# RMSNorm with SiLU: a first block of four rows, last blocks of four and two, and the first store behind the squares of block 1

## The chip, the cores and the metric

The kernel runs on one core of a Trainium2 chip. The time is device microseconds for one execution; a lower one is better. A core has five engines that run side by side: TensorE (PE), VectorE (DVE), ScalarE (ACT), GpSimd (POOL) and SyncE (SP). Data moves between the chip's main memory (HBM) and the on-chip memory (SBUF) through 16 DMA engines, which all transfers of the core share. A transfer is issued by an instruction on an engine's queue; here SP issues all loads and ACT all stores.

## The reference

The input x is 8 x 1024 x 2048 in float32, that is 8192 rows of 2048 numbers (8 KB each, 67.1 MB in all). Each row is divided by its root mean square, multiplied by gamma, and passed through SiLU. The output has the size of the input.

```python
def reference(x, gamma, eps):
    rms = np.sqrt(np.mean(x ** 2, axis=-1, keepdims=True) + eps)
    out = gamma * x / rms
    return (out * (1 / (1 + np.exp(-out)))).astype(np.float32)
```

## The kernel before

The 8192 rows are 64 for each of the 128 partitions. They are cut into blocks: a block of J rows covers 128 x J consecutive rows of x, and partition p holds J consecutive ones, so that one partition's piece is J x 8 KB of contiguous memory. Before the change there are eleven blocks: ten of six rows (48 KB per partition, 6 MB in all) and one of four (32 KB, 4 MB).

A pool of four buffers of six rows holds the blocks (`BUFS = 4`). `load(b)` (line 59) issues one transfer on SP, `store(b, j0, j1)` (line 66) one on ACT. Every block is computed in place and stored from the buffer it was loaded into. A load into a buffer thus waits until the store of the block that was in it has completed: load b + 4 waits for store b.

`work(b)` is one block's computation, in program order:

- ACT squares the first half of the rows and sums each (line 73, a Square with an accumulated output into `ss`); DVE does the same for the other half by a multiply and reduce (line 75).
- ACT takes the square root of the mean square plus eps for all rows of the block (line 80); DVE takes the reciprocal (line 85).
- For each row DVE multiplies by gamma, held on every partition as `g` (line 83), and ACT applies Silu with the reciprocal as its scale (line 86). DVE's half of the rows goes first.
- ACT issues the store of the block; in the last block in two halves, the first of them as soon as its rows are done. Then SP issues the load of block b + 4.

[...]

At the start the loads of blocks 0, 1 and 2 are issued. Gamma comes in as four pieces on ACT's queue into the fourth buffer, is spread over the partitions by four matmuls (line 111) and copied to `g` (line 113); then the load of block 3 goes into that fourth buffer (its load waits for the matmuls).

The order on each engine is the program's order: the whole kernel is under a manual schedule. So what ACT does before a store is issued is all that stands before it in the program, and a load on SP stands behind all loads issued before it.

Of the kernel before, what the change touches and what calls it, by code (L numbers as in the profile page):

```python
# [1 line left out]

# [4 lines left out]

ACT = mybir.ActivationFunctionType
ALU = mybir.AluOpType


@with_exitstack
def kernel(
    ctx: ExitStack,
    tc: tile.TileContext,
    x: bass.AP,
    gamma: bass.AP,
    eps: bass.AP,
    out: bass.AP,
):  # L20

    nc = tc.nc
    P = nc.NUM_PARTITIONS
    f32 = mybir.dt.float32
    x2 = x.flatten_outer_dims()
    o2 = out.flatten_outer_dims()  # L30
    n, d = x2.shape
    JMAX, BUFS = 6, 4
    blks = []
    r = 0
    while r < n:
        j = JMAX if n - r >= JMAX * P else 4
        blks.append((r, j))
        r += j * P
    nblk = len(blks)

    def rows_of(t, b):
        r0, J = blks[b]
        return t[r0:r0 + P * J, :].rearrange("(p j) d -> p (j d)", p=P, j=J)

    singles = ctx.enter_context(tc.tile_pool(name="singles", bufs=1))
    pool = ctx.enter_context(tc.tile_pool(name="pool", bufs=BUFS))
    small = ctx.enter_context(tc.tile_pool(name="small", bufs=2))
    psum = ctx.enter_context(tc.tile_pool(name="psum", bufs=1, space=bass.MemoryType.PSUM))

    g = singles.tile([P, d], f32)  # L50
    eps_t = singles.tile([P, 1], f32)
    ones = singles.tile([P, P], f32)
    junk_a = psum.tile([P, d], f32, name="junk_a")
    junk_v = psum.tile([P, d], f32, name="junk_v")
    blocks = {}

    def load(b):
        xt = pool.tile([P, JMAX * d], f32, name="xt")
        nc.sync.dma_start(out=xt[:, 0:blks[b][1] * d], in_=rows_of(x2, b))  # L59
        blocks[b] = xt  # L60

    def row(b, j):
        return blocks[b][:, j * d:(j + 1) * d]

    def store(b, j0, j1):
        nc.scalar.dma_start(out=rows_of(o2, b)[:, j0 * d:j1 * d], in_=blocks[b][:, j0 * d:j1 * d])  # L66

    def work(b):
        J = blks[b][1]
        A = J // 2  # L70
        ss = small.tile([P, JMAX], f32, name="ss")
        for j in range(A):
            nc.scalar.activation(out=junk_a, in_=row(b, j), func=ACT.Square, accum_out=ss[:, j:j + 1])  # L73
        for j in range(A, J):
            nc.vector.tensor_tensor_reduce(  # L75
                out=junk_v, in0=row(b, j), in1=row(b, j), scale=1.0, scalar=0.0,
                op0=ALU.mult, op1=ALU.add, accum_out=ss[:, j:j + 1])
        rms = small.tile([P, JMAX], f32, name="rms")
        rstd = small.tile([P, JMAX], f32, name="rstd")
        nc.scalar.activation(out=rms[:, 0:J], in_=ss[:, 0:J], func=ACT.Sqrt, scale=1.0 / d, bias=eps_t)  # L80
        order = list(range(A, J)) + list(range(A))
        for i, j in enumerate(order):
            nc.vector.tensor_mul(out=row(b, j), in0=row(b, j), in1=g)  # L83
            if i == 0:
                nc.vector.reciprocal(out=rstd[:, 0:J], in_=rms[:, 0:J])  # L85
            nc.scalar.activation(out=row(b, j), in_=row(b, j), func=ACT.Silu, scale=rstd[:, j:j + 1])  # L86
            if b == nblk - 1 and i == J - A - 1:
                store(b, A, J)
        if b == nblk - 1:
            store(b, 0, A)  # L90
        else:
            store(b, 0, J)
        if b + BUFS < nblk:
            load(b + BUFS)

    with tc.manual_schedule():


        Q = 4
        w = d // Q  # L100
        grow = pool.tile([P, JMAX * d], f32, name="xt")
        for b in range(BUFS - 1):
            load(b)
        nc.vector.memset(ones, 1.0)  # L104
        nc.vector.memset(eps_t, float(eps))  # L105
        nc.scalar.activation(out=junk_a[:, 0:1], in_=ones[:, 0:1], func=ACT.Square)  # L106
        nc.scalar.dma_start(out=grow[0:P:P // Q, 0:w],
                            in_=bass.AP(tensor=gamma.tensor, offset=gamma.offset, ap=[[w, Q], [1, w]]))
        for c in range(Q):
            k = c * (P // Q)  # L110
            nc.tensor.matmul(junk_v[:, c * w:(c + 1) * w], ones[k:k + 1, :], grow[k:k + 1, 0:w],  # L111
                             start=True, stop=True)
        nc.vector.tensor_copy(out=g, in_=junk_v)  # L113
        load(BUFS - 1)
        for b in range(nblk):
            work(b)


# [1 line left out]
_INS = ['x', 'gamma', 'eps']  # L120
_OUTS = [((8, 1024, 2048), 'float32')]

_NUMBERS = {'eps': 9.999999747378752e-06}


# [26 lines left out]
```

## Time and profile before

| | |
|---|---|
| median of 11 runs | 317.32 us (317.17 to 318.49) |
| the profiled execution | 317.3 us, of which the span of its instructions is 315.5 us |
| VectorE busy | 218.9 us, 69% of the span |
| ScalarE busy | 222.4 us, 70% of the span |
| gamma product, line 83 | 64 rows, 2277 ns each, 142.4 us |
| Silu, line 86 | 64 rows, 1996 ns each, 125.3 us |
| reduction on VectorE, line 75 | 32 rows, 2299 ns each; waits 59.8 us for loads |
| square on ScalarE, line 73 | 32 rows, 1882 ns each and 186 ns to read its sum; waits 56.6 us for loads |
| table loads on ScalarE | 11 before Sqrt and 11 before Silu, 1283 ns each |
| a load of 6 MB | median 35.1 us from issue to landing |
| a store of 6 MB | median 45.9 us from issue to landing |

The profile is one execution. Its span reaches from the first instruction to the last; the time has about 2 us more, outside the span. "Busy" is the share of the span in which an engine worked. In rows with a square bracket, the bracket holds the time for which the engine was idle before this instruction, and what released it. The DMA share of a stretch is the mean busy share of the 16 DMA engines, and the rate beside it is what they moved; both are counted by whole packets, of up to 48 KB here, so short stretches swing (a share can pass 1).

### The profile page before, as it was taken

The page shows a single profiled execution, that of the slowest core. Times are in us where ns is not written, and L with a number is a line of the kernel's source. Part 1 is how long each engine was busy: PE and PEld are TensorE (multiplying, and loading weights), DVE is VectorE, ACT ScalarE, POOL GpSimd, SP SyncE. Part 2 cuts the span into 40 slices and gives each one's busy share as a digit, 9 for nine tenths or more (in the row PEclk, how much of TensorE's full clock was granted, in tenths as well). Part 3 has the DMA queues.
Part 4 walks back from the last instruction along what each step waited for, and adds up shares of the span by engine and source line. Part 5 has one row for each costly group of instructions (what it writes and reads, how often), then busy time and mean ns, then how long its engine had stood idle before and what let it go on. Part 6 is the DMA issues. An engine that isn't in the chain of part 4 may idle for free.

```text
span 315.5 us, 421 instructions
## 1 busy us (share of the span) xinstructions
PE 2.1 (1%) x8; PEld 0.5 (0%) x8; DVE 218.9 (69%) x142; ACT 222.4 (70%) x163; POOL 0.2 (0%) x4
## 2 busy tenths in 40 slices
PE   0200000000000000000000000000000000000000
PEld 0000000000000000000000000000000000000000
DVE  0269998989989099539926990996299269959100
ACT  1068999999999289738956892898289568978400
POOL 0000000000000000000000000000000000000000
DMA  8999999999999999999999999999999999999997
GB/s 306 480 411 411 474 349 461 399 436 461 400 450 442 405 455 436 405 461 430 405 486 411 418 474 405 424 467 405 436 455 405 442 430 436 415 459 437 405 422 310
DMA packets 3323, 134.25 MB, mean 426 GB/s; under 512 B 372, under 2 KB 372, under 8 KB 376
## 3 DMA queue, kind: packets, MB, share of 16 engines
q1 hardware_dynamic: 1584, 67.11, 49.8%
q10 hardware_dynamic: 1736, 67.12, 49.2%
q14 instruction: 3, 0.02, 0.0%
HBM read 67.12 MB, written 67.11 MB: 425 GB/s over the span
## 4 chain that ended last, share of the span: by engine, by line
another core or an unknown queue 36%; DMA 31%; DVE 15%; ACT 9%; issue 1%; SPq 0%; ACTq 0%; DVEq 0%
DMA out_dram<-xt 16%; DMA xt<-in_x_dram 15%; DVE xt L83 11%; ACT xt L86 4%; DVE junk_v L75 4%; ACT junk_a L73 3%; ACT L80 1%; SPq L59 0%; ACT L86 0%; ACTq L66 0%; ACT rms L80 0%; DVE rstd L85 0%; DVE ss L75 0%; DVEq L75 0%
## 5 line engine op out<-in xcount | busy, mean ns | idle before, releaser
L83 DVE TENSOR_TENSOR xt<-xt,g 128x2048 f32<-128x2048 f32 x64 | 142.4, 2277 | 0.0
L86 ACT ACTIVATE xt<-xt,rstd 128x2048 f32<-128x2048 f32 x64 | 125.3, 1996 | 4.4 <-DVE xt L83 3.2
L75 DVE CUSTOM_DVE_ANT_0 junk_v<-xt 128x2048 f32<-128x2048 f32 x32 | 73.6, 2299 | 60.6 <-DMA xt<-in_x_dram 59.8
L73 ACT ACTIVATE junk_a<-xt 128x2048 f32<-128x2048 f32 x32 | 60.2, 1882 | 58.5 <-DMA xt<-in_x_dram 56.6
L80 ACT ACT_TABLE_LOAD x11 | 14.1, 1283 | 8.9 <-DVE ss L75 8.9
L86 ACT ACT_TABLE_LOAD x11 | 14.1, 1283 | 0.5 <-issue 0.3
L113 DVE COPY g<-junk_v 128x2048 f32<-128x2048 f32 x1 | 2.3, 2290 | 10.0 <-PE junk_v L111 10.0
L73 ACT ACTIVATION_READ_ACCUMULATOR junk_a<-xt 128x1 f32 x32 | 6.0, 186 | 0.0
L75 DVE DVE_READ_ACCUMULATOR2_ANT ss<- 128x1 f32 x32 | 4.5, 140 | 0.0
L85 DVE RECIPROCAL rstd<-rms 128x6 f32<-128x6 f32 (+1 forms) x11 | 2.0, 184 | 2.9 <-ACT rms L80 2.9
L80 ACT ACTIVATE rms<-ss,eps_t 128x6 f32<-128x6 f32 (+1 forms) x11 | 3.3, 300 | 0.1
L111 PE MATMUL junk_v<-xt,ones 1*128 1x512 f32 x8 | 2.1, 1132 | 8.8 <-DMA xt<-in_gamma_dram 8.8
L106 ACT ACT_TABLE_LOAD x1 | 1.3, 1283 | 0.7 <-PEq L133 0.7
L104 DVE MEMSET ones<- 128x128 f32 x1 | 0.2, 165 | 0.8 <-PEq L133 0.8
L111 PEld LDWEIGHTS junk_v<-xt,ones 1*128 1x128 f32 x8 | 0.5, 304 | 8.8 <-issue 8.8
L106 ACT ACTIVATE junk_a<-ones 128x1 f32<-128x1 f32 x1 | 0.2, 174 | 0.0
L133 POOL MEMSET const-bfloat16-1.0<- 128x1 bf16 x1 | 0.1, 102 | 0.0
L133 POOL MEMSET const-uint8-127<- 128x1 uint8 x1 | 0.1, 102 | 0.0
L133 POOL MEMSET const-float32-1.0<- 128x1 f32 x1 | 0.1, 99 | 0.0
L133 POOL MEMSET const-float32-0.0<- 128x1 f32 x1 | 0.1, 98 | 0.2 <-issue 0.2
L105 DVE MEMSET eps_t<- 128x1 f32 x1 | 0.1, 59 | 0.0
## 6 DMA issues: line engine op xcount, KB each, us to landing
xt<-in_x_dram SPq DMA_DIRECT2D x10, 6144.0 KB, 35.1
out_dram<-xt ACTq DMA_DIRECT2D x10, 6144.0 KB, 45.9
xt<-in_x_dram SPq DMA_DIRECT2D x1, 4096.0 KB, 30.3
out_dram<-xt ACTq DMA_DIRECT2D x2, 2048.0 KB, 18.8
xt<-in_gamma_dram ACTq DMA_DIRECT2D x1, 8.0 KB
```

The lines of the kernel that those rows point to most:

```text
L73: nc.scalar.activation(out=junk_a, in_=row(b, j), func=ACT.Square, accum_out=ss[:, j:j + 1])
L75: nc.vector.tensor_tensor_reduce(out=junk_v, in0=row(b, j), in1=row(b, j), scale=1.0, scalar=0.0, op0=ALU.mult, op1=ALU.add, accum_out=ss[ ...
L80: nc.scalar.activation(out=rms[:, 0:J], in_=ss[:, 0:J], func=ACT.Sqrt, scale=1.0 / d, bias=eps_t)
L83: nc.vector.tensor_mul(out=row(b, j), in0=row(b, j), in1=g)
L85: nc.vector.reciprocal(out=rstd[:, 0:J], in_=rms[:, 0:J])
L86: nc.scalar.activation(out=row(b, j), in_=row(b, j), func=ACT.Silu, scale=rstd[:, j:j + 1])
L104: nc.vector.memset(ones, 1.0)
L105: nc.vector.memset(eps_t, float(eps))
L106: nc.scalar.activation(out=junk_a[:, 0:1], in_=ones[:, 0:1], func=ACT.Square)
L111: nc.tensor.matmul(junk_v[:, c * w:(c + 1) * w], ones[k:k + 1, :], grow[k:k + 1, 0:w], start=True, stop=True)
L113: nc.vector.tensor_copy(out=g, in_=junk_v)
L133: nc = _bacc.Bacc("TRN2", target_bir_lowering=False, num_devices=1)
```

## The change

The cut into blocks becomes four rows, then nine times six, then four, then two: twelve blocks instead of eleven. The store of block 0 is no longer issued at the end of `work(0)`, but in `work(1)`, behind ACT's squares of block 1; the load of block 4, which needs block 0's buffer, moves with it. The last block is stored in one piece. Nothing changes in how a row is computed.

```diff
     JMAX, BUFS = 6, 4
-    blks = []
-    r = 0
-    while r < n:
-        j = JMAX if n - r >= JMAX * P else 4
-        blks.append((r, j))
-        r += j * P
+    nj = n // P
+    js = [4] + [JMAX] * ((nj - 4 - 6) // JMAX) + [4, 2]
+    blks = [(P * sum(js[:b]), j) for b, j in enumerate(js)]
+    assert sum(js) == nj
     nblk = len(blks)
...
         for j in range(A):
             nc.scalar.activation(out=junk_a, in_=row(b, j), func=ACT.Square, accum_out=ss[:, j:j + 1])
+        if b == 1:
+            store(0, 0, js[0])
+            load(BUFS)
         for j in range(A, J):
             nc.vector.tensor_tensor_reduce(
...
             nc.scalar.activation(out=row(b, j), in_=row(b, j), func=ACT.Silu, scale=rstd[:, j:j + 1])
-            if b == nblk - 1 and i == J - A - 1:
-                store(b, A, J)
-        if b == nblk - 1:
-            store(b, 0, A)
-        else:
+        if b > 0:
             store(b, 0, J)
-        if b + BUFS < nblk:
-            load(b + BUFS)
+            if b + BUFS < nblk:
+                load(b + BUFS)
```

## The prediction

> **What bounds the kernel now.** I read the page's totals first, then its slices, then what SyncE's queue waits for, then the rates of chosen stretches, then the last instructions.
>
> ```profile
> span 315.5 us, 421 instructions
> DMA  8999999999999999999999999999999999999997
> q1 hardware_dynamic: 1584, 67.11, 49.8%
> q10 hardware_dynamic: 1736, 67.12, 49.2%
> HBM read 67.12 MB, written 67.11 MB: 425 GB/s over the span
> ```
>
> q1 carries the loads, q10 the stores. Their packets took 49.8 + 49.2 = 99.0% of the 16 DMA engines' span: 312.3 us of 315.5. ScalarE is busy 70% and VectorE 69%, so neither can be the bound on average; the question is only where DMA is not at its rate. The stretches tell that (columns: stretch, length, busy time of PE, PEld, DVE, ACT, POOL, then clock, DMA share, GB/s):
>
> ```profile
> 0.00:1.50 1.50, 0.00 (x0) 0.00 (x0) 0.17 (x2) 0.77 (x1) 0.20 (x4) 1.00 0.00 0
> 1.50:4.00 2.50, 0.00 (x0) 0.00 (x0) 0.00 (x0) 0.69 (x2) 0.00 (x0) 1.00 1.03 315
> 18.00:38.00 20.00, 0.00 (x0) 0.00 (x0) 19.53 (x13) 18.06 (x14) 0.00 (x0) 1.00 1.00 433
> 41.00:50.00 9.00, 0.00 (x0) 0.00 (x0) 7.95 (x8) 8.66 (x9) 0.00 (x0) 1.00 0.98 366
> 120.00:240.00 120.00, 0.00 (x0) 0.00 (x0) 85.24 (x54) 86.72 (x63) 0.00 (x0) 1.00 1.01 436
> 254.00:278.00 24.00, 0.00 (x0) 0.00 (x0) 20.29 (x13) 20.67 (x15) 0.00 (x0) 1.00 0.99 429
> 282.00:312.00 30.00, 0.00 (x0) 0.00 (x0) 11.17 (x7) 12.31 (x9) 0.00 (x0) 1.00 0.99 426
> 314.00:315.50 1.50, 0.00 (x0) 0.00 (x0) 0.00 (x0) 0.00 (x0) 0.00 (x0) 1.00 0.00 0
> ```
>
> Loads alone run at 433 GB/s (18 to 38), loads and stores together at 436 (120 to 240), stores alone at 426 (282 to 312). Short stretches swing by a packet or two per engine, so I take 433 for all. Then the 134.2 MB are worth 310.0 us. The rest of the 315.5 is 1.5 us before the first packet, 1.5 us after the last, 2.5 x (433 - 315) / 433 = 0.7 us of slow start, and 9 x (433 - 366) / 433 = 1.4 us just after the first store is issued at 40.83; 0.4 us is rounding and engines that end unequally. These small terms are all that a schedule change can win without fewer bytes.
>
> ```profile
> SPq L59 <- DMA out_dram<-xt: 235.6, 7, 64.0
> 277.90 0.34 ACTq L66 DMA_DIRECT2D out_dram<-xt  x1
> 279.62 1.88 ACT L73 ACTIVATE junk_a<-xt 128x2048 f32<-128x2048 f32 x1 [1.75 <-DMA xt<-in_x_dram]
> 291.28 0.34 ACTq L66 DMA_DIRECT2D out_dram<-xt  x1
> 295.59 0.34 ACTq L66 DMA_DIRECT2D out_dram<-xt  x1
> ```
>
> SyncE's loads wait for stores to free a buffer, seven times: a ring of four buffers around a full DMA. At the end the last load has landed by 279.62, the last store is issued at 295.59, and packets end near 314: 18.4 us of stores, of which the last (2 MB) is 2.1 / 433 = 4.8 us. The store queue thus had 13.6 us of other work when the last store joined it.
>
> **The change, part by part.** One row of all partitions is 1.05 MB, 2.42 us at 433 GB/s.
>
> *Bytes and pieces.* The bytes stay: 64 rows in, 64 out. Loads go from 11 to 12, stores stay at 12 (eleven blocks with the last in two halves, then twelve blocks). The trace's packet records give 1.815 us for 48 KB, 1.213 for 32 KB and 0.611 for 16 KB: 0.301 per 8 KB and 0.009 for each packet. One more load is 8 more data packets for each of the 16 engines, and one semaphore packet of 0.009: 9 x 0.009 = +0.1 us.
>
> *A first block of four rows.* Its load lands two rows earlier: 18.3 - 4.8 = 13.4 us; g is ready then (its copy ends at 13.25). Before's last block has four rows, and went from landing (279.62) to the end of its last Silu (295.59) in 16.0 us, 0.4 of it a store issue: 15.6, so block 0 is done at 29.0. This frees no DMA time, as loads run on behind it.
>
> *The store moved behind block 1's squares.* Block 1 lands at 13.4 + 14.5 = 27.9. Its three squares on ScalarE take 6.1 us (41.23 to 47.3 in before), so store 0 is issued at about 29.0 + 6.1 = 35.1 instead of 40.83. Being moved past three squares costs that store 6.1 us and saves the squares the 0.35 us of its issue; VectorE's share of block 1 starts at 27.9 regardless. Load 4 stays behind store 0's completion on SP, which nothing else needs meanwhile. Nobody waits for the store at this point: loads 0 to 3 are 22 rows, 53.2 us of work for the DMA from 1.5 on, so to about 55 even without any store. Block 1 is VectorE's: 23.5 us in before from its first reduction (38.69) to its store (62.18), so store 1 goes out at 27.9 + 23.5 = 51.4, before the loads run dry. Store 0 in before took 34.5 us, 8 pairs of packets (8 x 3.63 = 29.0) and 5.5 besides; now 8 x (1.815 + 1.213) + 5.5 = 29.7, so load 4 goes out near 65 instead of 75.35. From there each load follows the one before by 29.0 us, as on SP in before. Cost and gain here: nothing, because one queue or the other is always full. If that cover failed, each microsecond of it would be lost.
>
> *The first-store loss of 1.4 us* comes with the first join of stores to loads, of which there is still one. Nothing in before shows it for a 32 KB store. Bounds: it is gone (-1.4), or it is doubled (+1.4). The nearest row is the start of before's own first store, also onto a full load queue; I take no change. The slow start of 0.7 us likewise: an effect of the first packets, bounded by 0 and 1.4, taken as it is.
>
> *Twelve blocks.* One more block adds two table loads (2 x 1.28), a Sqrt (0.30) and a reciprocal (0.18): 3.2 us for ScalarE and VectorE together. A block of six takes them 21 us of a 29 us period; they wait 56.6 and 59.8 us for loads. Hidden; without that cover 3.2 us.
>
> *The tail.* Load 8 goes out at 65 + 4 x 29 = 181, load 10 near 239; load 11 follows store 7, one shorter round later (eight 48 KB stores beside 32 KB loads and what is left of load 9), near 264. Its eight 16 KB packets run between 48 KB stores, 8 x 2.43 = 19.4, plus the 5.5 seen above: it lands near 289. Two rows need one reduction (2.4), table loads and Sqrt (3.0) and two Silus (3.9): store 11 goes out by 299. Packets end near 314; its own 4.8 us leave 10 us of earlier stores as cover, against 13.6 now. Splitting the last store is dropped at no cost for the same reason.
>
> The sum: 315.5 + 0.1 = 315.6 span. The profiled execution took 317.3, 1.8 more than its span, so 317.4; the median of before, 317.32, is that same time.
>
> [...]
>
> **The rivals.**
> - *The join costs more (slower).* The small first store meets load 2 or 3 at 35 us; if the loss of 41 to 50 comes twice, for instance again with the first six-row store, the end moves by 1.4 to 318.8. It decides from a loss of 0.6 us on. For it: the dip to 366 is real and unexplained. Against it: no later store shows it (436 over 120 us).
> - *The tail runs dry (slower).* Block 11 would have to be 10 us late on ScalarE; then each further microsecond counts. One whole block of four before it is 16 us and done near 286. Were it to land together with block 11, the store would go out at 289 + 16 + 9 = 314 and end 4.8 + 1.5 later: span 320, time 322. Against it: 20 us lie between their landings.
> - *Earlier mixing pays (faster).* The stores start 5.7 us earlier and the stretch of stores alone shrinks by some 10 us. If mixed traffic were truly faster by 436 to 426, 2.3%, that is 15.7 x 2.3% = 0.4 us: 317.0. With the join loss gone as well, 315.6. Against it: the records' 1.815 us for a 48 KB packet holds in all three stretches.
>
> **How the numbers follow.** About 0.2%, 0.6 us, is what a measurement can tell from no change. No change: 0.75, with 317.4 as time. A larger join or start loss: 0.10; a dry tail or another stall: 0.03. A join or start loss that shrinks by more than half: 0.12. So faster 0.12, same 0.75, slower 0.13. The range goes half of the join loss down and somewhat over half up, 316.7 to 318.2, and leaves out nearly two in ten.
>
> **What would show it.** Right: DMA shares of the queues that sum to 99% of a span near 315.6; the first store issued near 35; SP's waits on stores ending 29 us apart; the last load landed near 289, and 30 us of stores at 426 or more behind it. Wrong: a slice below 9 tenths in the DMA line other than the last, a second stretch below 400 GB/s over 8 us or more, or a start stretch below 300.

## The result, and the profile after

The changed kernel took 319.07 us (median of 13 runs, 318.19 to 321.01) against 317.47 (49 runs, 317.17 to 319.05): a ratio of 1.0057 over all these runs, with a 95% interval of 1.0045 to 1.0069 (the medians alone give 1.0050). The forecast was no change, 317.4 with a range to 318.2; the kernel is 1.6 us slower and lies outside. The profiled execution took 321.27 us, the longest seen, so what it shows is larger than in the median run. The ratios below leave out runs more than 1.5% above the fastest of their kernel: one of j2 (328.11 us) and one of h2 (335.05 us).

The page of the changed kernel:

```profile
span 319.5 us, 430 instructions
...
DMA  8999999999999999999999999999999999999992
...
q1 hardware_dynamic: 1728, 67.11, 49.2%
q10 hardware_dynamic: 1736, 67.12, 48.6%
```

The two queues sum to 97.8% of 319.5, that is 312.5 us of work for the mean DMA engine. Before it was 312.3. The work has not grown; the span has, and the last slice fell from 7 tenths to 2.

The order of events is near the forecast until the last load. From the timeline of the changed kernel (start, length, engine, line; the bracket is idle time before):

```profile
32.71 1.88 ACT L72 ACTIVATE junk_a<-xt 128x2048 f32<-128x2048 f32 x1
32.72 0.36 ACTq L65 DMA_DIRECT2D out_dram<-xt  x1
49.97 0.34 ACTq L65 DMA_DIRECT2D out_dram<-xt  x1
...
264.66 0.33 SPq L58 DMA_DIRECT2D xt<-in_x_dram  x1
...
292.65 0.34 ACTq L65 DMA_DIRECT2D out_dram<-xt  x1
296.86 1.88 ACT L72 ACTIVATE junk_a<-xt 128x2048 f32<-128x2048 f32 x1 [4.24 <-DMA xt<-in_x_dram]
306.12 0.34 ACTq L65 DMA_DIRECT2D out_dram<-xt  x1
```

The first store is issued at 32.72 (35.1 forecast: in the trace ScalarE's queue issues it as the third square starts, at 32.71, not when it ends), the last load at 264.66 (264 forecast). The squares that wait for that load start at 296.86 instead of 289, and the last store went out at 306.12 instead of 299. DMA did not run dry:

```profile
282.00:310.00 28.00, 0.00 (x0) 0.00 (x0) 15.50 (x10) 19.26 (x14) 0.00 (x0) 1.00 1.00 431
```

The loss of time is in the last microseconds. Stretches of the changed kernel, then the same of the kernel before; the last two columns are the mean busy share of the 16 DMA engines and GB/s:

```profile
308.00:311.00 3.00, 0.00 (x0) 0.00 (x0) 0.00 (x0) 0.00 (x0) 0.00 (x0) 1.00 1.01 431
311.00:313.00 2.00, 0.00 (x0) 0.00 (x0) 0.00 (x0) 0.00 (x0) 0.00 (x0) 1.00 0.84 360
313.00:315.00 2.00, 0.00 (x0) 0.00 (x0) 0.00 (x0) 0.00 (x0) 0.00 (x0) 1.00 0.19 82
315.00:317.00 2.00, 0.00 (x0) 0.00 (x0) 0.00 (x0) 0.00 (x0) 0.00 (x0) 1.00 0.11 49
317.00:319.00 2.00, 0.00 (x0) 0.00 (x0) 0.00 (x0) 0.00 (x0) 0.00 (x0) 1.00 0.06 25
```

```profile
311.00:313.00 2.00, 0.00 (x0) 0.00 (x0) 0.00 (x0) 0.00 (x0) 0.00 (x0) 1.00 0.97 418
313.00:315.00 2.00, 0.00 (x0) 0.00 (x0) 0.00 (x0) 0.00 (x0) 0.00 (x0) 1.00 0.16 66
315.00:317.00 2.00, 0.00 (x0) 0.00 (x0) 0.00 (x0) 0.00 (x0) 0.00 (x0) 1.00 0.00 0
```

A share of 0.11 over 2 us is 0.11 x 16, less than two engines. In the changed kernel most engines finish by about 313, and two go on for some 5 us. The packet records show how a transfer is cut: 128 data packets, one for each partition, and 16 packets of 4 bytes, one at the end of each engine's part. In the kernel before, the packets can be strung, each starting as another ends, into 16 chains of 184 data packets each, so every engine has the same fixed part, eight packets of each transfer. In the changed kernel the others stand idle while the last two work on: nothing takes over their rest, and the kernel ends with the slowest.

The 4-byte packets also date each engine's part of a transfer (us; the median of the 16 engines, and the last of them):

| landing of | before, median | before, last | after, median | after, last |
|---|---|---|---|---|
| load 2 | 50.87 | 51.48 | 45.75 | 48.25 |
| load 5 | 137.89 | 139.06 | 129.81 | 134.92 |
| load 8 | 224.89 | 226.06 | 216.83 | 223.02 |
| the last load | 278.07 | 279.24 | 289.42 | 296.50 |
| the last store | 313.54 | 314.34 | 313.07 | 318.30 |

The median engine kept to the forecast: 289.42 for the last load (289 forecast), 313.07 for the end (near 314 forecast). The work that waits for a load starts when its last engine is done (squares at 296.86). The lag of the last engine grew from 2.5 us, at the first landing behind the first store, to 7.1; in before it is never above 1.2 for a load.

The packet records of the trace also allow an exact sum for the mean engine, from the first data packet to the last: the packets at their usual length (1.8155, 1.213 and 0.611 us), what packets took beyond that, and idle time, nearly all of it waiting at the end for the slowest.

| profiled execution | usual length | beyond it | idle | first to last packet |
|---|---|---|---|---|
| before | 310.0 | 2.1 | 0.6 | 312.6 |
| after | 310.0 | 2.1 | 4.4 | 316.6 |

So nothing is lost on average: the packets' excess is the same 2.1 us, but in the changed kernel it is uneven. The last engine, which has no idle time at the end, has some 6.6 us (316.6 - 310.0). Of the mean excess, 0.6 us comes after 70 us, in single longer packets; in before 0.05.

### The profile page after: what moved, and what is told of

It reads as the page before. It is cut to its first block, busy times and chain, and to the rows that moved or that the text cites. A ratio compares the mean times of both kernels' runs of the same rounds, so it can differ in the third digit from the quotient of the medians.

```text
span 319.5 us, 430 instructions
## 1 busy us (share of the span) xinstructions
PE 2.1 (1%) x8; PEld 0.5 (0%) x8; DVE 219.2 (69%) x143; ACT 225.0 (70%) x166; POOL 0.2 (0%) x4
## 4 chain that ended last, share of the span: by engine, by line
DMA 62%; DVE 16%; another core or an unknown queue 9%; ACT 6%; issue 1%; SPq 0%; ACTq 0%
DMA xt<-in_x_dram 32%; DMA out_dram<-xt 30%; DVE xt L85 12%; DVE junk_v L77 4%; ACT xt L88 3%; ACT junk_a L72 2%; ACT L82 0%; ACT L88 0%; SPq L58 0%; ACT rms L82 0%; DVE ss L77 0%; DVE rstd L87 0%; ACTq L65 0%; ACTq L82 0%
## 5 line engine op out<-in xcount | busy, mean ns | idle before, releaser
L82 ACT ACT_TABLE_LOAD x12 | 15.4, 1283 | 10.2 <-DVE ss L77 10.1
L88 ACT ACT_TABLE_LOAD x12 | 15.4, 1283 | 1.1 <-issue 1.0
L82 ACT ACTIVATE rms<-ss,eps_t 128x6 f32<-128x6 f32 (+2 forms) x12 | 3.6, 299 | 0.1
L87 DVE RECIPROCAL rstd<-rms 128x6 f32<-128x6 f32 (+2 forms) x12 | 2.1, 179 | 0.2 <-ACT rms L82 0.2
```

## The experiments

**Which part of the change.** Four kernels, each with one part.

`e1_cut_alone`: the new cut, with the store of block 0 at the end of its own work.

```diff
-        if b == 1:
-            store(0, 0, js[0])
-            load(BUFS)
...
-        if b > 0:
-            store(b, 0, J)
-            if b + BUFS < nblk:
-                load(b + BUFS)
+        store(b, 0, J)
+        if b + BUFS < nblk:
+            load(b + BUFS)
```

> The new cut 4, 9 x 6, 4, 2, with store 0 and load 4 at the end of block 0's work. In the profile of the changed kernel two of the sixteen DMA engines end some 5 us after the others, all with the same bytes. Theory A (the four-row first block puts loads and stores out of step, and engines that are then out of step lose time): stays slow, ratio 1.003 to 1.008, last packets 3 to 6 us behind the mean engine. Theory B (the moved store alone does it): 1.000 with an end within 1 us as before. Theory C (the small last blocks do it): slow as well, like A; the runs e3 and e4 tell A from C.

`e2_moved_store_alone`: the kernel before, with `store(0, 0, blks[0][1])` and `load(BUFS)` behind the squares of block 1.

> The cut of before, but store 0 and load 4 behind the squares of block 1. Theory A: 1.000 (no more than 0.1% off), since block 0 still lands late and the stores still fill the queue. Theory B: 1.003 to 1.008, with engines that lag at the end. Theory C: 1.000.

`e3_first_block_alone`: the kernel before with `js = [4] + [JMAX] * 10`.

> Cut 4, 10 x 6, everything else as before (store 0 in its own place, last store in halves). Theory A: 1.003 to 1.008, DMA share falling off over the last 4 to 6 us. Theory B and theory C: 1.000.

`e4_last_blocks_alone`: as e1 with `js = [JMAX] * 9 + [4, 4, 2]`.

> Cut 9 x 6, 4, 4, 2, store 0 in its own place, last block stored whole. Theory C: 1.003 to 1.008. Theory A and theory B: 1.000 to 1.001.

Measured: e1 1.0035 (1.0013 to 1.0057), e2 1.0171 (1.0141 to 1.0202), e3 1.0020 (0.9996 to 1.0043), e4 1.0025 (1.0008 to 1.0043). Moving the store alone is by far the worst, three times the whole change; but it goes out at 45.10 there and at 32.72 in the changed kernel, so the parts can't be added up. None of the three theories fits all four. B names the worst part, with too small a size, and has e1 at 1.000. A and C fit e1, but have e2 at 1.000, and the 1.003 to 1.008 that A names for e3 and C for e4 lie above what was measured. The cuts cost 0.20 to 0.35%, with e3 not distinct from nothing. The runs of e1 fall into two groups, eight from 317.31 to 318.64 and four from 319.73 to 320.38, and those of e3 too, eight up to 317.67 and four from 319.23: the same program sometimes ends as fast as before and sometimes 3 us later.

In e2 the end looks as in the changed kernel (stretches, columns as above):

```profile
311.00:313.00 2.00, 0.00 (x0) 0.00 (x0) 0.00 (x0) 0.00 (x0) 0.00 (x0) 1.00 0.81 344
313.00:315.00 2.00, 0.00 (x0) 0.00 (x0) 0.00 (x0) 0.00 (x0) 0.00 (x0) 1.00 0.36 156
315.00:317.00 2.00, 0.00 (x0) 0.00 (x0) 0.00 (x0) 0.00 (x0) 0.00 (x0) 1.00 0.12 49
317.00:319.00 2.00, 0.00 (x0) 0.00 (x0) 0.00 (x0) 0.00 (x0) 0.00 (x0) 1.00 0.06 25
319.00:321.00 2.00, 0.00 (x0) 0.00 (x0) 0.00 (x0) 0.00 (x0) 0.00 (x0) 1.00 0.08 33
```

About one engine is at work in the last 4 us (0.06 x 16 and 0.08 x 16).

**Place or moment.** The store of e2 is issued at 45.10 instead of 40.83. These kernels keep it in its place and delay it by squares of g, whose results nothing uses:

```diff
         else:
+            if b == 0:
+                for m in (2048, 2048, 2):
+                    nc.scalar.activation(out=junk_a[:, 0:m], in_=g[:, 0:m], func=ACT.Square)
             store(b, 0, J)
```

with (2048, 2048, 2) in g3, (2048, 2) in g1 and (1024, 2) in g2.

> The kernel before, with two squares of g on ScalarE (results unused) and a third of two columns between block 0's last Silu and its store; the store is then issued about 4.1 us later, as in e2, but stays in its place in the program. Theory D (what counts is when the first store joins the load stream: where it falls, a few DMA engines lose a packet more than the others, and an engine behind the others keeps losing): 1.012 to 1.020 as e2. Theory B (the place behind block 1's squares, with the engines' work beside it, counts): 1.000 to 1.002.

> As g3 with one full square of g: the store is issued about 2.0 us later than before, 1.1 load packets of 1.815 us. Theory D: a time between that of before and that of e2, with another number of lagging engines; no number can be given beyond 0.998 to 1.020. Theory B: 1.000.

> As g3 with one square of 1024 columns: about 1.0 us later, half a load packet. Theory D: differs from g1 if the place within a packet counts, 0.998 to 1.020; theory B: 1.000.

Measured: g3, issued at 44.51, 1.0183 (1.0156 to 1.0211), as e2; g1, at 42.61, 1.0151 (1.0134 to 1.0167); g2, at 41.71, 1.0013 (1.0004 to 1.0023). The place isn't needed for the loss, the moment is enough: between 41.71 and 42.61 lie 4.5 us of kernel time. A store issued 1.8 us late, behind which the loads still have some 18 us of work (24 rows of 2.42 us from 2.2 on), costs 4.8 us.

The squares of g also delay what ScalarE does next: g1 issues its second store at 64.02, before at 62.18. That the loss needs this later work is ruled out by e2, whose second store goes out at 61.97; there the first store moved and the time still rose by 1.7%.

g1 also shows a second form of the loss. The stretch from 50 to 90, first of g1, then of the kernel before:

```profile
50.00:90.00 40.00, 0.00 (x0) 0.00 (x0) 38.11 (x24) 38.47 (x29) 0.00 (x0) 1.00 1.01 414
```

```profile
50.00:90.00 40.00, 0.00 (x0) 0.00 (x0) 38.90 (x25) 38.48 (x29) 0.00 (x0) 1.00 1.00 432
```

The engines are as busy, yet move 4% less: many packets are longer (72 of 337 above 1.9 us, 22 above 2.4, for 1.815). By the sum above g1 lost 4.5 us beyond the usual length and 2.8 idle; g3 3.0 and 5.9; e2 2.7 and 7.2. Two kernels that come further on, j1 and k3, have this second form as well: 3.2 and 1.3, and 3.9 and 3.0. Some 1.6 and 1.5 us of theirs lie between 70 and 90, where load 4 joins the stores after 8 us (j1) and 19 us (k3) without a load packet: j1 moved 359 GB/s from 70 to 80 (before 423), k3 324 from 75 to 85 (before 398).

**Does an engine that is behind fall further back?** h1 gives two of the sixteen engines a packet more at the start; h2, as its control, was to give all sixteen one more.

```diff
+        nc.scalar.dma_start(out=grow[1:3, 0:JMAX * d], in_=x2[0:2 * JMAX, :].rearrange("(p j) d -> p (j d)", p=2, j=JMAX))
         for c in range(Q):
```

(h2: `grow[1:17, ...]` from 16 pieces.)

> The kernel before, with one additional load at the start of two partitions of 48 KB each (into the buffer of gamma, ahead of load 3, which overwrites it): one packet of 1.815 us more for two of the sixteen DMA engines, nothing for the others. If an engine that is behind stays as far behind (no growth): 1.8 us more at the end, ratio 1.0057. If it keeps losing (theory A and D): more than that, 1.008 to 1.018. If the engines level out: below 1.003.

> The control to h1: the kernel before with sixteen partitions of 48 KB loaded additionally at the start, one packet of 1.815 us for every one of the sixteen DMA engines. All are later by the same, none falls behind. If it is the difference between engines that cost h1 its 1.9%: 1.8 us more, ratio 1.004 to 1.008. If any additional load there costs that much: 1.015 to 1.022. The store now joins one packet earlier in the stream of loads, so by theory D a spread could come in besides.

Measured: h1 1.0194 (1.0176 to 1.0213), h2 1.0456 (1.0425 to 1.0487). Neither settles the question. In h1 the two additional packets took 3.0 and 3.1 us instead of 1.815, the first load landed 2.7 us later on its last engine, and the first store went out at 43.85, among the moments that g1 and g3 show to be bad by themselves. In h2 the additional load was slow itself:

```profile
4.00:20.00 16.00, 2.09 (x8) 0.55 (x8) 2.29 (x1) 0.00 (x0) 0.00 (x0) 1.00 1.11 179
```

179 GB/s for 16 us where the kernel before has above 400: the sixteen pieces, all to partitions 1 to 16, took 2.7 to 8.4 us each, and packets of the loads beside them up to 8.4. That is no control. The traces show both: in the changed kernel the last engine's lag grows from load to load (2.5 to 7.1 us), in before it is at most 1.2, and in e2 most of it is there at 98 us (10.4 at that store's landing, 11.9 at most, 8.5 at the end). No run shows by itself that an engine that is behind must fall further back.

**The moment in the new cut.** i1 puts the store behind two of the three squares of block 1; i2, i3, j1 and j2 put 0, 1, 2 and 3 full squares of g and one of two columns ahead of it (the diff is i3's).

```diff
         if b == 1:
+            for m in (2048, 2):
+                nc.scalar.activation(out=junk_a[:, 0:m], in_=g[:, 0:m], func=ACT.Square)
             store(0, 0, js[0])
```

> The changed kernel with the store of block 0 behind two of the three squares of block 1, not behind all: issued about 2 us earlier, near 30.7. Theory D (the moment of the join decides how far the DMA engines spread): a time that differs from the changed kernel's 1.0057, somewhere in 0.999 to 1.018. If the moment doesn't matter in this cut, 1.004 to 1.007 as for the changed kernel.

> The changed kernel with a square of two columns of g (result unused) ahead of the moved store, so that it goes out when the third square has ended, about 2 us later, near 34.8. Theory D: differs from 1.0057, within 0.999 to 1.018; else 1.004 to 1.007.

> As i2 with one more full square of g ahead: about 4 us later, near 36.8. Theory D: differs from 1.0057, within 0.999 to 1.018; else 1.004 to 1.007.

> The changed kernel with two full squares of g and one of two columns ahead of the moved store: issued near 38.5, 6 us later than in the changed kernel. So far its cut gave 1.0080 at 30.8, 1.0057 at 32.7, 1.0035 at 34.9 and 1.0023 at 36.7. If the join alone makes the loss, 0.999 to 1.002. If the four-row blocks cost something by themselves, a floor of 1.002 or more stays.

> As j1 with three full squares: near 40.4. If the join alone makes the loss, a time that may be as low as j1 or higher again (the old cut rose from 1.001 to 1.015 within a microsecond); a floor from the blocks: at least 1.002.

| first store issued | kernel | ratio | 95% interval |
|---|---|---|---|
| 28.64 | e1 | 1.0035 | 1.0013 to 1.0057 |
| 30.77 | i1 | 1.0080 | 1.0057 to 1.0103 |
| 32.72 | the changed kernel | 1.0057 | 1.0045 to 1.0069 |
| 34.89 | i2 | 1.0035 | 1.0023 to 1.0047 |
| 36.66 | i3 | 1.0023 | 1.0013 to 1.0033 |
| 38.51 | j1 | 1.0086 | 1.0053 to 1.0118 |
| 40.58 | j2 | 1.0174 | 1.0141 to 1.0206 |

With the same blocks, the same transfers and the same bytes, the time moves between 1.0023 and 1.0174 with the issue of the first store. In e1, i1, the changed kernel and i2 the second store stays at 49.97 to 50.14, so up to there only the first one moved; i1 and i2 lie apart beyond their intervals. So the moment counts in this cut too. In i3, j1 and j2 the second store moves along, to 55.83 in j2. Its best here is still 0.2% above the kernel before; whether that is the blocks' own cost isn't settled by seven moments. j2 ends as e2 does, with few engines:

```profile
315.00:317.00 2.00, 0.00 (x0) 0.00 (x0) 0.00 (x0) 0.00 (x0) 0.00 (x0) 1.00 0.15 66
317.00:319.00 2.00, 0.00 (x0) 0.00 (x0) 0.00 (x0) 0.00 (x0) 0.00 (x0) 1.00 0.10 41
319.00:321.00 2.00, 0.00 (x0) 0.00 (x0) 0.00 (x0) 0.00 (x0) 0.00 (x0) 1.00 0.06 25
```

**What about the moment.** Later still in the old cut, with 4, 3, 5 and 7 full squares (j3, k1, k2, k3, in this order):

> The kernel before with four full squares of g and one of two columns ahead of store 0: issued near 48.4. If any late join is bad in this cut, 1.015 or more; if the loss depends on where in the load stream the store arrives, it can be anywhere, also near 1.000, as long as the queue of loads doesn't run dry.

> The kernel before with three full squares of g and one of two columns ahead of store 0: issued near 46.5. Theory E: what counts is where in the running load of 14.5 us (eight packets for each engine) the store is issued; so far the first and the middle part cost little, the last quarter 0.9 to 1.8%, in both cuts. Loads 2 and 3 of the old cut run from 32.2 to 46.7 and from 46.7 to 61.2. 46.5 is at the very end of load 2: 1.010 to 1.020. If the loss goes with lateness alone between 42 and 48, falling from 45 on: 1.005 to 1.012.

> As k1 with five full squares: near 50.5, 0.26 of the way through load 3. Theory E: as the new cut at 0.29 and 0.42, 1.004 to 1.010. If the loss was tied to 42 to 46 us: 1.000.

> As k1 with seven full squares: near 54.6, 0.54 of the way through load 3. Theory E: 0.999 to 1.004, as in the middle of a load. If late joins are bad because the loads run low (they end near 61): 1.005 or more.

| first store issued | kernel | ratio | 95% interval |
|---|---|---|---|
| 40.83 | before | 1 | |
| 41.71 | g2 | 1.0013 | 1.0004 to 1.0023 |
| 42.61 | g1 | 1.0151 | 1.0134 to 1.0167 |
| 44.51 | g3 | 1.0183 | 1.0156 to 1.0211 |
| 45.10 | e2 | 1.0171 | 1.0141 to 1.0202 |
| 46.35 | k1 | 1.0029 | 1.0013 to 1.0045 |
| 48.58 | j3 | 1.0005 | 0.9990 to 1.0019 |
| 50.22 | k2 | 1.0016 | 1.0002 to 1.0030 |
| 54.41 | k3 | 1.0084 | 1.0055 to 1.0114 |

Lateness is not it: 8 us late costs nothing (j3), 2 to 4 us late costs 1.5 to 1.8%. j3 ends as the kernel before does:

```profile
311.00:313.00 2.00, 0.00 (x0) 0.00 (x0) 0.00 (x0) 0.00 (x0) 0.00 (x0) 1.00 0.99 426
313.00:315.00 2.00, 0.00 (x0) 0.00 (x0) 0.00 (x0) 0.00 (x0) 0.00 (x0) 1.00 0.12 49
315.00:317.00 2.00, 0.00 (x0) 0.00 (x0) 0.00 (x0) 0.00 (x0) 0.00 (x0) 1.00 0.00 0
```

Theory E, the position within the running load, fell: the end of load 2 (k1) should have cost 1 to 2% and cost 0.3, the middle of load 3 (k3) should have cost at most 0.4 and cost 0.8, and a quarter of the way in (k2) should have cost 0.4 to 1.0 and cost 0.2. The other reading named for k3, loads that run low, has its number right (0.5 or more); but k2 too has 14 us without a load packet, and no such loss.

What orders most of the runs was seen only afterwards, in the packet records: how long after the first packet of a store the first packet of the next load comes, once the ring of buffers has settled (110 to 240 us). It comes mostly in steps of about a packet. Three or four packets (5.4 to 7.3 us): before, g2, e4, i2, i3, j3, k1 and k2, all at 1.0035 or less, but k3 too, which is slow, and j2, which is slow and goes from four to six. Five to nine packets (9.2 to 15.4): j1, the changed kernel (10.9), g1, g3, i1, e2 and h1, all at 1.0057 or more. Eleven (about 20.5): e1 and e3, 1.0035 and 1.0020. Each offset is that of one execution; those of e1 and e3 took 317.31 and 317.17 us and belong to the lower of their two groups of runs. In every one but j2 the offset keeps to within 0.3 us from 110 to 240. That it is the cause isn't shown: two of nineteen kernels go against it (h2 left out), no run was made that sets it by itself, and why engines come to lag at some moments and not at others stays open.

## Why the prediction was wrong

- **What bounds the kernel**: right. DMA, and nothing else, sets the end; the work of the mean engine is 312.5 us after and 312.3 before.
- **Bytes and pieces, +0.1**: right. The usual length of all packets is 310.02 us against 309.96.
- **Order of events**: right for landings, stores and loads to within 3.5 us until the last load. That landing and the last store came 7 to 8 us late, which used up 7 of the 10 us of earlier stores that the forecast had as cover; so DMA did not run dry.
- **The first-store loss of 1.4 us**: on the mean engine this shrank; packets at the join were 0.9 us longer in sum, against 1.2 in before. The bounds of -1.4 and +1.4 were put on the wrong quantity, the mean.
- **"Cost and gain here: nothing, because one queue or the other is always full"**: this is the step that failed, for the moved store. In the changed kernel the queues were full, and yet the last engine ended 5.2 us behind the median one. The term "0.4 us is rounding and engines that end unequally" was carried over without a reason; the idle time at the end, 0.6 us in before, measured 4.4 us in the profiled execution, and that is 3.8 of the 4.0 us by which this span is longer. Sixteen engines were added up as one server at 433 GB/s, and the slice with 7 tenths at the end was read as a fixed cost. The signs of being wrong left out this last slice, the one place where the loss shows. How much of the median's 1.6 us is due to the store's moment and how much to the cut stays open, and so does why the engines lag.
- **The rivals**: "the join costs more" named the right place and came near with 318.8, but that is luck: its mechanism, the dip of the rate coming twice, did not happen in the changed kernel (402 GB/s from 30 to 41, 466 from 41 to 50, 428 from 70 to 90); it did in j1 and k3. The forecast could have asked why the runs of before already scatter upwards, to 318.49; that their engines end apart isn't shown, as one execution of before has a profile.

## What to carry to other kernels

Where every transfer is cut in fixed parts over the DMA engines, as here, a kernel at the DMA's rate ends with its slowest engine: look at the DMA share of the last microseconds. A share of one or two sixteenths there (0.11 over 2 us in the changed kernel) can be engines that lag. A change that moves no bytes can still cost 1 to 2% by the moment of one store, so measure an early or late store at several moments, and in many runs, before a reason is given for it. Here no version beat the kernel before, whose first store happens to go out at a good moment; in g1 a delay of that store by 1.8 us lost 1.5%.

## What was not expected of the hardware

- A shift of the first store by 0.9 us (41.71 to 42.61) changed the kernel by 4.5 us, with the same transfers (what ScalarE does behind it moved by as much); a further shift to 48.58 gave it back.
- The same program takes different times from run to run, in two groups: e1 had runs at 317.31 and at 320.38. That this too is engines that end apart isn't shown, as only an execution of the lower group has a profile.
- Sixteen 48 KB pieces, all to partitions 1 to 16 beside the first load, held the rate at 179 GB/s for 16 us (h2).
